# Nine row buffers instead of six and a later cut of the gather schedule in a hybrid decoder layer

## Chip, cores and metric

One Trainium2 chip, one core of it. The metric is the device time of one execution in microseconds; lower is better. Several executions are timed and their median is given; one more is profiled.

## The reference

One layer over 1024 tokens of width 1024, in float32: a token mixer (a short convolution group and a chunked gated DeltaNet group), cross-attention into 256 memory tokens, and a PEER channel mixer. The last one matters here. For each token it picks 8 x 16 = 128 of 16384 single-neuron experts and computes

```
u = expert_u[it]; v = expert_v[it]        # it: 128 expert numbers of each token
act = gelu(einsum("td,ted->te", xt, u))
y   = einsum("te,ted->td", gt * act, v)   # gt: 128 gates of each token
```

A final RMSNorm of the sum with the residual closes the layer.

## The kernel before

**Blocks and chunks.** The 1024 tokens are 8 blocks of 128. The mixer, the attention and the choice of experts run by chunks: `ca` (blocks 0 and 1), `cb` (2 to 5) and `cc` (6 and 7). The PEER mixer has two ways. Blocks 2 to 5 go the *dense* way (`densify`, lines 1025 to 1066, and `dense`, lines 1068 to 1143): a table of gates over all 16384 experts is made for each block by one-hot products on DVE and PE (the "tables"), and then all of `u_t` and `expert_v` are streamed past the 512 tokens. Each streamed tile `wraw` is split by ACT (`whi`, line 242) and DVE (`wlo`, line 244) for three matmuls (lines 248 to 250). Blocks 0, 1, 6 and 7 go by *gathers*: one indirect DMA of POOL's (line 918, or 964) fetches one expert row for each of 128 tokens, 128 x 4 KB, into one buffer `g`. The pool `gp` holds `NG` = 6 of these buffers, for U rows and V rows alike, and for the three tiles that `finish` (lines 992 to 1005) uses.

**What is done with a gathered row.** U rows are multiplied with the token and summed on DVE (line 935). V rows of blocks 1, 6 and 7 are weighted and added up on DVE (line 1020, the first on ACT, line 1018). V rows of block 0 go through PE (`gather_p`, line 971, into a PSUM bank `acc` that is copied to an SBUF slot `t_s` at line 983 and then to DRAM). `finish` loads the residual and the final gain, adds (999), squares on ACT (1001), takes an inverse root (lines 229 to 235, 12 small DVE instructions) and scales (1004).

```
915:  for k in range(NSLOT):
916:      ...
917:      g = gp.tile([P, D], F32, name="g")
918:      nc.gpsimd.indirect_dma_start(out=g, ...)
1016: for k, g in gathered("expert_v", r.ii, LV):
1020:     stt(y, g, a[:, k:k + 1], y, op0=OP.mult, op1=OP.add)
```

**What sets the order.** The parts are generators that yield after each step, and `merge` interleaves several of them in proportion to given weights. `gathers(0)` yields 3 steps for closing block 0's routing, 131 for block 0's U sums merged with block 1's closing, 256 for block 1's U sums merged with block 0's V rows (the close of block 0 is traced at the end of these), and 128 for block 1's V sums. The numbers `G1` to `G5` say how many of these steps are traced beside each part of the other work; what is left is merged with the dense stage, together with the 518 steps of blocks 6 and 7, against `PACE` = 517 dense steps:

```
1209: run(merge((steps(ga, G4), G4), (qb, 32), (steps(rest, C4), C4)))
1210: run(merge((steps(ga, G5), G5), (tables2, T5), (rest, 195 - C4)))
1213: run(merge((chain(ga, at('PG3', gathers(6))), 1036 - G1 - G2 - G3 - G4 - G5), (at("PD", dense(2 * P)), PACE)))
```

`tables2` closes the routing of blocks 2 to 5 (`route_close`) and makes their tables; `rest` is the mixer, the attention and `queries` of chunk `cc`, in that order. The order of tracing is a priority: a scheduler then sets the order of each engine's instructions, and pulls traced-later work forward where its operands and its buffer slots are there. Slots of a pool are given out in the order of tracing. The slots `t_s` (`NSLIP` = 4) are used by `best_keys` in `queries`, by `route_close` and by the copy at line 983. From the queries of `cb` on, `psum()` gives out the four `ps` banks only.

Of the kernel before, what the change touches and what calls it, by code (L numbers as in the profile page):

```python
# [39 lines left out]
CSTART = [sum(CAND[:r]) for r in range(16)]  # L40
NCAND = sum(CAND)
NSLIP, CLOSE, PACE = 4, 3, 517
G1, G2, G3, G4, G5 = 98, 90, 107, 17, 60
A5 = -1
C4, T5 = 61, 92
NSHORT, NRAW, NHI, NLO, NG, LU, LV, VD = 6, 3, 2, 2, 6, 1, 1, 194
PG1, PG2, PG3, PT, PR, PD = 100, -25, 0, 0, 0, 0


# [1205 lines left out]

# [10 lines left out]
```

## Time and profile before

| | us |
|---|---|
| median of 3 runs | 3342.78 (3332.52 to 3343.3) |
| profiled execution | 3335.89 |
| its span, first to last instruction | 3334.1 |
| PE busy in the span | 2784.7 (84%) |
| DVE busy | 2693.7 (81%) |
| ACT busy | 1339.8 (40%) |
| POOL busy | 1324.6 (40%) |

The share of 16 DMA engines' time that packets took is 44.3% for POOL's queue (the gathers) and 30.0% for SP's queue. A share over the whole span mixes stages with different limits, so the stages have to be read one by one. "Idle time, and what ended it" says for an engine which instruction of another engine or which DMA released the next instruction.

### The profile page before, as it was taken

To read this page: it belongs to the slowest core of one execution; us is meant where nothing else is said; L and a number is where in the kernel's file an instruction comes from. 1 tells how busy PE (TensorE), PEld (TensorE's weight loads), DVE (VectorE), ACT (ScalarE), POOL (GpSimd) and SP (SyncE) were. 2 spreads that over 40 slices of the span, in tenths; PEclk is the share of its full clock that TensorE was granted. 3 is DMA by queue.
4 is the path that set the end of the run, shared out by engine and by line. 5 is a ranking of instruction groups with operands and counts; after the bars stand their busy time and mean duration, and the time that the engine had idled before them with its cause. 6 is when DMAs were issued, how large, how long until landed. Compare 5 with 4: busy or idle time off the path is not lost.

```text
span 3334.1 us, 42650 instructions
## 1 busy us (share of the span) xinstructions
PE 2784.7 (84%) x14826; PEld 2307.0 (69%) x14826; DVE 2693.7 (81%) x5527; ACT 1339.8 (40%) x2367; POOL 1324.6 (40%) x1028
## 2 busy tenths in 40 slices
PE   7898588877888877466777999999999999999950
PEld 7887466666555656465656888888888888888840
DVE  6654899978655788997668999888888888887888
ACT  5444333322232323334443554444444444444430
POOL 0000046746545441000000456556655555665665
PEclk9999788989998888788788999999999999999975
DMA  4344368959988884113455889999999999999998
GB/s 166 113 147 140 120 233 302 354 184 324 328 309 306 308 291 155 64 77 143 154 190 188 297 307 363 347 344 346 345 336 342 348 348 349 343 339 339 348 329 315
DMA packets 325495, 890.34 MB, mean 267 GB/s; under 512 B 27424, under 2 KB 96672, under 8 KB 321184
## 3 DMA queue, kind: packets, MB, share of 16 engines
q0 software_dynamic: 147456, 536.94, 44.3%
q1 hardware_dynamic: 177824, 350.69, 30.0%
q8 instruction: 116, 1.90, 0.2%
q14 instruction: 99, 0.81, 0.1%
HBM read 838.77 MB, written 48.76 MB: 266 GB/s over the span
## 4 chain that ended last, share of the span: by engine, by line
PE 43%; DVE 3%; issue 2%; DMA 1%; ACT 1%; POOL 1%; SPq 0%; POOLq 0%; DVEq 0%; ACTq 0%
PE ps L248 7%; PE ps L249 7%; PE ps L250 7%; PE po L248 7%; PE po L250 7%; PE po L249 7%; DMA g<-expert_v,g_ii 1%; POOL g L918 1%; DVE unit L1053 0%; DMA d_s<-kmd 0%; PE ps L1059 0%; DVE g_y L1020 0%; DVE wlo L244 0%; ACT whi L242 0%; DVE unit L1050 0%
## 5 line engine op out<-in xcount | busy, mean ns | idle before, releaser
L918 POOL DMA_INDIRECT g<-expert_u,g_ii x512 | 666.4, 1302 | 898.9 <-DVE t_s L820 434.4
L918 POOL DMA_INDIRECT g<-expert_v,g_ii x384 | 518.5, 1350 | 930.8 <-ACT g L1001 536.0
L242 ACT ACTIVATE whi<-wraw 128x1024 fp32r<-128x1024 f32 x452 | 479.9, 1062 | 836.0 <-PE ps L249 413.5
L244 DVE TENSOR_TENSOR wlo<-wraw,whi 128x1024 fp32r<-128x1024 f32 x452 | 552.4, 1222 | 321.7 <-ACT whi L242 319.4
L935 DVE SCALAR_TENSOR_TENSOR g<-g,xn 128x1024 f32<-128x1024 f32 x512 | 617.4, 1219 | 121.0 <-DMA g<-expert_u,g_ii 111.7
L250 PE MATMUL ps<-unit,wlo 128*128 128x512 f32 (+1 forms) x1784 | 653.3, 367 | 39.4 <-DVE wlo L244 39.3
L248 PE MATMUL ps<-unit,whi 128*128 128x512 f32 (+1 forms) x1784 | 659.1, 370 | 13.7 <-ACT whi L242 5.5
L249 PE MATMUL ps<-unit,whi 128*128 128x512 f32 (+1 forms) x1784 | 651.6, 365 | 0.0
L1020 DVE SCALAR_TENSOR_TENSOR g_y<-g,g_a,g_y 128x1024 f32<-128x1024 f32 x381 | 488.1, 1281 | 20.1 <-DMA g<-expert_v,g_ii 12.7
L249 PE MATMUL po<-wlo,unit 128*128 128x512 f32 x1136 | 444.0, 391 | 0.0
L250 PE MATMUL po<-whi,unit 128*128 128x512 f32 x1136 | 443.9, 391 | 0.0
L250 PEld LDWEIGHTS ps<-unit,wlo 128*128 128x128 f32 x1784 | 350.3, 197 | 98.6 <-DVE wlo L244 45.0
L248 PEld LDWEIGHTS ps<-unit,whi 128*128 128x128 f32 x1784 | 351.6, 197 | 76.7 <-ACT whi L242 11.0
L249 PEld LDWEIGHTS ps<-unit,whi 128*128 128x128 f32 x1784 | 351.5, 197 | 50.0 <-issue 0.8
L248 PE MATMUL po<-whi,unit 128*128 128x512 f32 x1136 | 383.1, 391 | 0.0
L249 PEld LDWEIGHTS po<-wlo,unit 128*128 128x128 f32 x1136 | 214.1, 188 | 48.3 <-issue 2.7
L250 PEld LDWEIGHTS po<-whi,unit 128*128 128x128 f32 x1136 | 214.0, 188 | 46.8 <-issue 2.5
L248 PEld LDWEIGHTS po<-whi,unit 128*128 128x128 f32 x1136 | 214.0, 188 | 45.8 <-issue 1.1
L1113 ACT ACTIVATE unit<-po 128x512 f32<-128x512 f32 x256 | 152.6, 597 | 150.1 <-PE po L250 144.8
L964 POOL DMA_INDIRECT g<-expert_v,g_y x128 | 139.4, 1089 | 161.3 <-DVE g L935 57.5
L1100 ACT ACTIVATE po<-unit 128x512 f32<-128x512 f32 x248 | 144.5, 605 | 0.0
L1059 PE MATMUL ps<-unit 128*128 128x128 f16 x1024 | 86.8, 239 | 52.3 <-DVE unit L1053 38.7
(391 smaller groups left out, 4053.1 us busy)
## 6 DMA issues: line engine op xcount, KB each, us to landing
wraw<-u_t SPq DMA_DIRECT2D x128, 512.0 KB, 7.1
wraw<-expert_v SPq DMA_DIRECT2D x128, 512.0 KB, 7.0
wraw<-w_in SPq DMA_DIRECT2D x84, 512.0 KB, 4.6
gd<-unit SPq DMA_DIRECT2D x32, 1024.0 KB, 5.9
unit<-gd SPq DMA_DIRECT2D x32, 1024.0 KB, 15.1
wraw<-w_out SPq DMA_DIRECT2D x24, 512.0 KB, 4.2
wraw<-w_xq SPq DMA_DIRECT2D x24, 512.0 KB, 4.4
wraw<-w_xo SPq DMA_DIRECT2D x24, 512.0 KB, 4.9
```

What stands on the lines that cost most here:

```text
L242: act(hi, raw, AF.Copy)
L244: tt(lo, raw, hi.bitcast(F32), op=OP.subtract)
L248: nc.tensor.matmul(ps, lh, rh, start=first, stop=False, skip_group_check=open_)
L249: nc.tensor.matmul(ps, lh, rl, start=False, stop=False, skip_group_check=open_)
L250: nc.tensor.matmul(ps, ll, rh, start=False, stop=last, skip_group_check=open_)
L918: nc.gpsimd.indirect_dma_start(out=g, out_offset=None, in_=I[table], in_offset=bass.IndirectOffsetOnAxis(ap=ii[:, k:k + 1], axis=0))
L935: stt(g, g, 1.0, xn, op0=OP.mult, op1=OP.mult, accum_out=r.a[:, k:k + 1])
L964: nc.gpsimd.indirect_dma_start(out=g, out_offset=None, in_=I["expert_v"], in_offset=bass.IndirectOffsetOnAxis(ap=iT[:, t:t + 1], axis=0))
L1020: stt(y, g, a[:, k:k + 1], y, op0=OP.mult, op1=OP.add)
L1059: nc.tensor.matmul(ps[:, u * P:(u + 1) * P], part[i][:, g, :, t], oj[:, g, :, t], start=i == 0, stop=i == 1)
L1100: act(pss[b], y[b][:, half * 512:(half + 1) * 512], AF.Copy)
L1113: act(y[b][:, half * 512:(half + 1) * 512], pss[b], AF.Copy)
```

## The change

`NG` goes from 6 to 9: nine buffers `g` of 4 KB in each partition. The scratch that holds the descriptors of dynamic transfers is given as 4096 bytes of each partition. `G5` goes from 60 to 130: 70 more steps of `gathers(0)` are traced beside the tables and the rest of chunk `cc`, and 70 fewer beside the dense stage (the weight 664 in line 1213 becomes 594). Nothing that is computed changes.

```
-G1, G2, G3, G4, G5 = 98, 90, 107, 17, 60
+G1, G2, G3, G4, G5 = 98, 90, 107, 17, 130
...
-NSHORT, NRAW, NHI, NLO, NG, LU, LV, VD = 6, 3, 2, 2, 6, 1, 1, 194
+NSHORT, NRAW, NHI, NLO, NG, LU, LV, VD = 6, 3, 2, 2, 9, 1, 1, 194
...
-    nc = bacc.Bacc("TRN2", target_bir_lowering=False, num_devices=1)
+    nc = bacc.Bacc("TRN2", target_bir_lowering=False, num_devices=1, dynamic_dma_scratch_size=4096)
```

## Rows read from the trace of the kernel before

**Rows 1.** Stages: start:end, us, busy us (instructions) by engine, clock, DMA share, GB/s

```profile
434.00:667.00 233.00, 189.78 (x821) 150.95 (x821) 230.61 (x449) 79.02 (x124) 153.26 (x114) 0.91 0.89 318
667.00:1290.00 623.00, 505.37 (x2867) 375.19 (x2868) 449.49 (x1208) 176.20 (x363) 303.87 (x274) 0.88 0.80 288
1290.00:1500.00 210.00, 128.57 (x1007) 118.89 (x1005) 196.96 (x690) 76.87 (x176) 0.00 (x0) 0.79 0.20 77
1500.00:1800.00 300.00, 209.17 (x1570) 175.06 (x1570) 218.86 (x524) 131.06 (x341) 0.00 (x0) 0.84 0.46 168
...
1826.00:3210.00 1384.00, 1382.66 (x6099) 1144.22 (x6098) 1174.47 (x1459) 673.72 (x970) 787.47 (x570) 1.00 0.95 340
3210.00:3334.00 124.00, 0.66 (x3) 0.19 (x2) 106.96 (x145) 6.83 (x12) 77.88 (x66) 0.51 0.87 314
```

The engines stand in the order PE, PEld, DVE, ACT, POOL.

**Rows 2.** DVE's largest group from 3210 on; the chain's last sum

```profile
L1020 DVE SCALAR_TENSOR_TENSOR g_y<-g,g_a,g_y 128x1024 f32<-128x1024 f32 x71 | 91.1, 1284 | 11.0 <-DMA g<-expert_v,g_ii 10.1
...
3322.59 1.30 DVE g_y L1020
```

**Rows 3.** Waits in 1826 to 3210: us in total, times, longest

```profile
DVE g_y L1020 <- DMA g<-expert_v,g_ii: 2.5, 3, 1.1
...
POOL g L918 <- DVE g_y L1020: 241.1, 164, 5.3
POOL g L918 <- DVE g L935: 201.0, 116, 5.4
```

**Rows 4.** POOL's timeline around 1286 to 1822: start, us, [idle before, releaser]

```profile
1286.20 0.94 POOL L918 DMA_INDIRECT g<-expert_v,g_ii  x1 [9.19 <-DVE p_top L820]
1822.15 0.94 POOL L918 DMA_INDIRECT g<-expert_v,g_ii  x1 [535.02 <-ACT g L1001]
```

**Rows 5.** Timelines of ACT and PE ahead of the dense stage

```profile
1807.47 0.60 ACT L983 ACTIVATE t_s<-ps 128x512 f32<-128x512 f32 x1 [10.06 <-DVE p_topi L821]
...
1808.12 3.90 PE L293 MATMUL ps<-call,unit 128*128 128x128 f32 x16 [11.34 <-ACT t_s L983]
```

**Rows 6.** Waits of PE, DVE and POOL in 667 to 1290

```profile
PE po L971 <- DMA g<-expert_v,g_y: 31.5, 13, 9.1
PE ps L971 <- DMA g<-expert_v,g_y: 25.2, 8, 6.3
...
DVE g L935 <- DMA g<-expert_u,g_ii: 109.9, 63, 9.7
...
POOL g L964 <- DVE g L935: 57.5, 27, 7.1
POOL g L918 <- PE ps L971: 53.9, 14, 8.6
```

**Rows 7.** DVE's groups of sums in 1826 to 3210: busy us, mean ns

```profile
L1020 DVE SCALAR_TENSOR_TENSOR g_y<-g,g_a,g_y 128x1024 f32<-128x1024 f32 x310 | 396.9, 1280 | 9.1 <-ACT g_y L1018 4.5 <-DMA g<-expert_v,g_ii 2.5
...
L935 DVE SCALAR_TENSOR_TENSOR g<-g,xn 128x1024 f32<-128x1024 f32 x256 | 307.9, 1219 | 0.0
```

**Rows 8.** DVE's timeline of a close, first and last large instruction and one small

```profile
3323.91 1.23 DVE L999 TENSOR_TENSOR g_y<-g_y,g 128x1024 f32<-128x1024 f32 x1
...
3326.58 0.15 DVE L230 TENSOR_SCALAR rs_y<-rs_x 128x1 int32<-128x1 int32 x1
...
3328.57 1.28 DVE L1004 SCALAR_TENSOR_TENSOR g_y<-g_y,f_r,g 128x1024 f32<-128x1024 f32 x1
```

**Rows 9.** DMA: POOL's queue (packets, MB, share); issues of U rows (median landing us)

```profile
q0 software_dynamic: 147456, 536.94, 44.3%
...
g<-expert_u,g_ii POOLq DMA_INDIRECT x512, 7.0
```

**Rows 10.** Two stretches of 200 us in the dense stage, columns as in rows 1

```profile
2000.00:2200.00 200.00, 200.00 (x884) 165.58 (x884) 173.69 (x183) 95.68 (x139) 112.98 (x86) 1.00 0.98 356
...
2800.00:3000.00 200.00, 200.00 (x884) 165.63 (x883) 166.23 (x192) 94.81 (x138) 117.91 (x85) 1.00 0.96 343
```

**Rows 11.** The chain in 1600 to 1826, one of its pieces: start, us, what

```profile
1732.04 3.61 DVE unit L1053 x6
```

## The prediction, made before the changed kernel was run

> **What bounds the kernel now.** I read the stage table first [rows 1]. It shows three kinds of time. From 1826 to 3210 us, while the dense stage runs, PE is busy 1382.66 of 1384 us at full clock: there PE is the bound, and whatever is taken off DVE or the DMA queues only shows at the end. After 3210 PE has nothing left, and 124 us go to block 7's expert sums and what closes the kernel. Before 1826 no engine is full throughout: DVE is in 434 to 667 and in 1290 to 1500; elsewhere PE and DVE wait for each other. In 1290 to 1800 (the "tables") POOL does nothing and the DMA engines are busy 20 to 46%, so gathers could run there; DVE has 300 - 218.9 = 81 us of idle time in 1500 to 1800 and only 13 before that.
>
> Next the end, in the groups of DVE and the chain [rows 2]: 71 sums of line 1020 start after 3210, 1.284 us each, with 10.1 us of waiting for gathers, so (91.1 + 10.1) / 71 = 1.43 us a sum. The last starts at 3322.59, and 11.5 us of block 7's close follow. This is a backlog: PE finished while 71 sums had not been done.
>
> Then, who waits for whom in the dense stretch [rows 3]: POOL waits 241.1 + 201.0 us for DVE to free a row buffer, while DVE waits only 2.5 us for a gather. The gathers are held back by buffers and by the place of the sums in DVE's order, not by late data.
>
> POOL's timeline says why the tables have no gathers [rows 4]: the first of block 1's V rows are fetched by 1286, and the next one's issue waits 535.02 us for line 1001, the close of block 0. That close comes late for a small reason [rows 5]: the copy at line 983 needs a `t_s` slot, traced behind all of `queries(cc)`, and waits for its top-16 work (line 821). The copy is also what PE's transposes for the dense stage wait for, 11.34 us, because the sum of block 0 holds one of the four `ps` banks until then.
>
> Last, the stretch with block 0's V rows on PE, 667 to 1290 [rows 6]: PE waits 31.5 + 25.2 = 56.7 us for gathers and DVE 109.9 us, while POOL waits 57.5 us for line 935 and 53.9 us for line 971 to free a buffer. Here six buffers are too few for the landing time.
>
> **The change, part by part.**
>
> *130 steps instead of 60 beside the tables.* The steps before this merge are 98 + 90 + 107 + 17 = 312. Steps 1 to 390 are block 0 and block 1's U sums with block 0's V rows (3 + 131 + 256); POOL has issued all of those gathers by 1286 already, as block 1's V rows are under way by then [rows 4]. So of the 70 added steps 18 change nothing, and 442 - 390 = 52 of block 1's V sums really move, with block 0's close before them. The close is now traced at step 78 of 130, in `cross(cc)` and ahead of `queries(cc)`, so its `t_s` slot should come free once the four `route_close` of the tables are through.
>
> What it adds in the tables: 52 sums of 1.28 us on DVE [rows 7] = 66.6 us, and the close, 1.23 + 1.28 us and 12 small ones of 0.15 [rows 8] = 4.3 us: 71 us. Its gathers cost POOL and DMA time that lies idle there [rows 1]; ACT gets three instructions more, with over half its time idle; the stores of line 987, the close's three loads and its store pass through SP, ahead of weight loads: a load that waits there for a free `g` would hold these up, which nine buffers make unlikely. DVE takes its queue in order, so each sum stands ahead of whatever `cross`, `queries` or `densify` has ready. Bounds: 0, if all 71 us fall into the 81 us of idle time; 71, if none does. A sum put into a gap delays the next instruction by half its length on average, 52 x 0.64 = 33 us; the `ps` bank that is returned early takes a little off. I take +30.
>
> What it removes: 52 sums from the backlog, 52 x 1.43 = 74 us, leaving 71 - 52 = 19 sums and a tail of 124 - 74 = 50 us. This holds if the dense stretch goes on doing 310 + 256 = 566 sums [rows 7]. Should block 1's other 76 sums also be pulled forward, tables and tail trade nearly one for one. Bounds 0 (nothing moves) and 74 + 27 = 101 (the 19 go too).
>
> The early copy of line 983 removes PE's wait ahead of the dense stage [rows 5]: -11; bounds -11 and 0, since DVE's top-16 work is also in the way there.
>
> *Nine buffers.* In 667 to 1290 a gather can be issued three buffers earlier. POOL runs 274 instructions in those 623 us, nearly all of them gathers, one per 2.3 us [rows 1]; three of them are 6.8 us, about what one takes to land (7.0 us [rows 9]), and the longest waits are 9.1 and 9.7 us. I let two thirds of PE's wait go: 56.7 x 0.67 = -38. DVE's 110 us I don't add, as PE is the busier there (505 against 449 us of 623). Bounds: 0, if the sums are merely moved forward to meet the rows as late as before, and -57. In 434 to 667 DVE is full (230.6 of 233), so buffers give nothing.
>
> In the dense stretch nine buffers could raise the pace. The DMA engines move 340 GB/s on average there [rows 1], 356 from 2000 to 2200 and 343 from 2800 to 3000 [rows 10]. To take in the remaining 19 sums, of 128 rows x 4 KB = 0.524 MB each, they would need 340 + 19 x 0.524 MB / 1384 us = 347. The later stretch is the usual one, so I leave the 19 in the tail. The Trainium skill (DMA: Bandwidth & Descriptors, "Where 436 GB/s comes from") puts the HBM side of one core at about 358 GB/s. By that rule 347 is within reach, the 19 sums go, and the sum below is 27 us lower; by the rows it stands.
>
> *A scratch of 4 KB.* It frees 12 KB of each partition, the three added buffers of 4 KB. Nothing in the trace shows the scratch as such. In the trace, six transfers in flight run freely with the present size; bounds for the smaller one are 0 and a limit below six, priced as a rival. I take 0, as no gather there waits for anything but a buffer or POOL's own issue [rows 3].
>
> **The sum.** 3334.1 - 38 (early buffers) + 30 (tables) - 11 (dense start) - 74 (tail) = 3241 us span, and 1.8 us outside it as in the profiled execution (3335.89): **3243 us**. That execution was 6.9 us under the median of the three runs (3342.78); a median like theirs would be 3250, inside every range here.
>
> **Rivals.**
>
> *Better: all of it.* The 19 sums also fit into the dense stretch (-27) and PE loses all 57 us of waiting (-19 more): 3243 - 46 = 3197. For it: POOL's 442 us of buffer waits in the dense stretch. Against: the rate of the DMA engines. Chance 0.10.
>
> *The tables pay in full.* The chain in the tables has stretches of DVE alone, such as six table products in a row [rows 11]; if it is DVE's throughout, all 71 us show, and the buffers give nothing early. 3334 - 74 - 11 + 71 + 2 = 3322, faster by 0.4%, at the edge. Chance 0.13.
>
> *The change does not do what it says.* The close of block 0 still gets its slot only behind `queries(cc)`, and block 1's sums stay after 1807. Only the early buffers act: 3336 - 38 = 3298. Against: its place in the trace order is now ahead of `queries`. Chance 0.07.
>
> *Slower: the sums run ahead of the DMA engines in the dense stage.* With nine buffers the sums are put into DVE's order as closely as DVE allows. It has 1384 - 1174 = 210 us free [rows 1], room for 168 sums, so 734 in 1384 us, one per 1.89 us: 278 GB/s of gathers. The stage's own loads are 340 - 566 x 0.524 / 1.384 = 126 GB/s; 404 together against 356 at best [rows 10]. DVE then waits for rows with `wlo` behind it, and PE starves. The 585 gathers (307 MB) get 278 / 404 of 356, 245 GB/s: 1252 us, in which PE does 1252 x 356 / 404 = 1103 us of its work; 281 more follow. The stage takes 1533 instead of 1384 us, the backlog is gone: 3243 + 149 - 27 = 3365. It decides once PE's idle time in the stage passes about 95 us. For it: the 442 us. Against: DVE waits 2.5 us for gathers now, and the merge spreads 594 steps evenly over the dense stage. Chance 0.09.
>
> *Slower: the scratch holds too few transfers.* If fewer than six fit, gathers in the dense stage slow from one per 2.45 us: with two in flight at 7.0 us, one per 3.5, and 585 of them take 2050 us behind a start at 1826: over 3870 us in all. The queue's row gives 147456 packets for 1024 gathers, 144 each, 9 on each of 16 engines [rows 9]. The Trainium skill (the same page, "The descriptor swizzle" and "Terms") also has 9 descriptors per engine and 16 bytes for one; a ring of 4096 bytes on each engine would then hold an estimated 28 transfers, so this page speaks against the rival, and no run here shows it yet. Chance 0.03.
>
> **How the numbers follow.** The forecast has the rest, 0.58, with 3205 to 3290 by its bounds. A run tells a difference of about 0.3% (10 us) here. Faster: 0.58 + 0.10 + 0.07 + 0.08 of the full-price case = 0.83; same: its other 0.05; slower: 0.09 + 0.03 = 0.12. The range, 3180 to 3325, holds the forecast, most of the better case, the full price and the case that nothing moves; it leaves out both slower ones.
>
> **What would show it.** Right: block 0's close (line 999) and sums of line 1020 well before 1800; about 52 fewer sums of line 1020 after the last matmul, and a tail of 30 to 55 us; PE's waits for gathers at line 971 under 25 us; no 11 us wait at line 293. Wrong: a stretch from 1290 to the dense start longer by over 70 us; a wait of DVE for gathers in the dense stage well over 2.5 us with PE under 1.00 busy; POOL's first gather after 1290 still behind line 1001 near 1820; gathers landing later than now with POOL held at its issue.

## The result, and the profile after

The changed kernel is slower: 3413.43 us (3407.48 to 3422.61, four runs) against 3343.04 for the kernel before beside it, a ratio of 1.0225 with an interval of 1.0205 to 1.0244. The forecast was 3243 us, with a range of 3180 to 3325, so it missed in sign and the time lies outside the range. In the profiled executions the spans are 3408.8 and 3334.1 us: 74.7 us to explain.

Two marks cut this difference into three pieces: ACT's first instruction of the dense stage and PE's last matmul. First the timelines (start, length, engine, line) of the kernel before:

```profile
1825.85 1.28 ACT L1088 ACT_TABLE_LOAD   x1
...
3210.27 0.39 PE L250 MATMUL po<-whi,unit 128*128 128x512 f32 x1
```

The same of the kernel after:

```profile
1881.64 1.28 ACT L1088 ACT_TABLE_LOAD   x1
...
3384.75 0.39 PE L250 MATMUL po<-whi,unit 128*128 128x512 f32 x1
```

The dense stage starts 1881.64 - 1825.85 = 55.8 us later. It takes 1503.1 us for 1384.4, 118.7 more. What follows PE's last matmul is 24.1 us for 123.8, 99.8 less. The sum is 55.8 + 118.7 - 99.8 = 74.7. So the tail went, as forecast and more, and was paid for twice.

The stage table of the kernel after (columns as in [rows 1]) answers to that group:

```profile
434.00:667.00 233.00, 177.49 (x682) 139.38 (x681) 231.23 (x414) 65.49 (x90) 170.34 (x128) 0.84 0.94 345
667.00:1290.00 623.00, 546.97 (x3150) 404.84 (x3149) 464.31 (x1264) 200.98 (x412) 294.80 (x260) 0.92 0.77 286
1290.00:1500.00 210.00, 112.64 (x895) 103.23 (x894) 199.81 (x673) 71.89 (x177) 0.00 (x0) 0.75 0.18 67
1500.00:1800.00 300.00, 168.68 (x1218) 139.67 (x1218) 289.37 (x428) 108.39 (x295) 159.34 (x107) 0.75 0.88 324
...
1882.00:3385.00 1503.00, 1431.69 (x6098) 1157.83 (x6096) 1117.98 (x1428) 672.95 (x971) 717.33 (x512) 0.98 0.81 293
3385.00:3409.00 24.00, 0.14 (x1) 0.00 (x0) 17.88 (x72) 6.17 (x12) 0.00 (x0) 0.56 0.27 110
```

From 1500 to 1800 DVE is busy 289.4 of 300 us (before 218.9), and PE does 1218 matmuls for 1570. DVE's groups of sums say how much came in there: first 1290 to 1882, then 1882 to 3385.

```profile
L1020 DVE SCALAR_TENSOR_TENSOR g_y<-g,g_a,g_y 128x1024 f32<-128x1024 f32 x124 | 158.5, 1278 | 1.4 <-DMA g<-expert_v,g_ii 0.5
...
L1020 DVE SCALAR_TENSOR_TENSOR g_y<-g,g_a,g_y 128x1024 f32<-128x1024 f32 x257 | 329.9, 1284 | 3.3 <-DMA g<-expert_v,g_ii 1.2
```

Before 1882 there are 124 of block 1's 127 sums, not 52. The timelines of ACT, DVE and POOL show what released them (in brackets the idle time before and its end):

```profile
1491.72 0.58 ACT L983 ACTIVATE t_s<-ps 128x512 f32<-128x512 f32 x1
...
1500.61 1.22 DVE L999 TENSOR_TENSOR g<-g 128x1024 f32<-128x1024 f32 x1 [2.30 <-DMA g<-hd]
...
1503.28 0.94 POOL L918 DMA_INDIRECT g<-expert_v,g_ii  x1 [272.60 <-ACT g L1001]
```

The close of block 0 moved from about 1820 to 1500, as the prediction read from the order of tracing, and POOL's wait for it fell from 535.02 us [rows 4] to 272.60. From then on nothing held block 1's sums but DVE.

Next, the dense stage. A stretch of 800 us well inside it compares best; before:

```profile
2000.00:2800.00 800.00, 800.00 (x3531) 662.43 (x3531) 665.59 (x812) 383.67 (x557) 466.05 (x340) 1.00 0.97 347
```

After:

```profile
2000.00:2800.00 800.00, 749.07 (x3155) 601.85 (x3154) 698.07 (x872) 342.98 (x498) 545.97 (x388) 0.97 0.99 364
```

388 gathers for 340, and 3155 matmuls for 3531: 10.6%, or 85 of 800 us, are lost. 51 us of them are idle time of PE; the other 34 are PE's busy time per matmul, which grew. The granted clock, 0.97 on average for 1.00, makes some 22 us of these (0.03 x 749); the other 12 the profile does not explain. The DMA engines are busy 0.99 of the time at 364 GB/s. The waits of 1882 to 3385 (in total, times, longest) name what PE stands at:

```profile
ACT ps L1088 <- PE ps L250: 242.7, 73, 5.0
...
POOL g L918 <- DVE g_y L1020: 130.1, 109, 7.6
...
POOL g L918 <- DVE g L935: 66.2, 54, 3.9
...
PE po L248 <- ACT whi L242: 40.3, 17, 5.3
...
ACT whi L242 <- DMA wraw<-expert_v: 26.1, 13, 5.4
...
PE ps L250 <- DVE wlo L244: 17.8, 24, 3.2
...
DVE g L935 <- DMA g<-expert_u,g_ii: 3.5, 2, 2.5
```

POOL's 442 us of waiting for buffers [rows 3] are down to 196. PE waits for the two halves of the weight tiles. ACT, which makes the first half, waits for the tiles themselves too, but for 26.1 us where it was 18.7 before, so this wait alone does not explain the loss. DVE still hardly waits for a gather. The chain from 2100 to 2900 has five weight loads among its pieces, 92 us in all (before, it has PE's matmuls alone), for instance:

```profile
2204.57 19.40 DMA wraw<-expert_v
...
2405.16 18.36 DMA wraw<-expert_v
...
2647.78 20.57 DMA wraw<-expert_v
```

From 2000 to 2900 the median tile of `expert_v` lands in 7.9 us (before 7.0); these are the late ones.

Late tiles are the smaller part of it, though. The timelines of ACT and PE show wait by wait what a late `whi` stood behind. Of PE's 51 us of idle time from 2000 to 2800, 13 follow a tile that had only just landed:

```profile
2668.43 1.06 ACT L242 ACTIVATE whi<-wraw 128x1024 fp32r<-128x1024 f32 x1 [3.56 <-DMA wraw<-expert_v]
...
2669.54 2.07 PE L248 MATMUL po<-whi,unit 128*128 128x512 f32 x4 [5.29 <-ACT whi L242]
```

Some 36 follow a `whi` that had to wait its turn on ACT. Its tile had landed (in PE's waits for `whi`, 1.8 to 11 us before, once 0.1), but in ACT's queue it stands behind the gelu of line 1088, or the copy of line 1113, of the tile that PE is still working on. ACT waits for PE to end that tile, and PE then waits for ACT:

```profile
2077.57 0.58 ACT L1088 ACTIVATE ps<-ps 128x512 f32<-128x512 f32 x1 [4.86 <-PE ps L250]
2078.06 1.05 ACT L242 ACTIVATE whi<-wraw 128x1024 fp32r<-128x1024 f32 x1
...
2079.16 1.19 PE L248 MATMUL po<-whi,unit 128*128 128x512 f32 x4 [1.63 <-ACT whi L242]
```

Before, from 2000 to 2800, the next tile's `whi` always stands ahead of these:

```profile
2323.47 1.06 ACT L242 ACTIVATE whi<-wraw 128x1024 fp32r<-128x1024 f32 x1 [2.01 <-PE ps L249]
2324.44 0.58 ACT L1088 ACTIVATE ps<-ps 128x512 f32<-128x512 f32 x1
```

In the same 800 us the changed kernel's queue has 24 places where it stands behind. So nine buffers changed the written order of ACT's queue as well as that of DVE's. Why the scheduler wrote it so, no run shows.

Behind 3000 all gathers are done, the stage runs at 874 matmuls per 200 us with the DMA engines at 119 GB/s to the end: the gathers were hurried through a stage that would have had room for them.

### The profile page after: what moved, and what is told of

Its sections match the earlier page's. It is cut to its first block, busy times and chain, and to the rows that moved or that the text cites. A ratio compares the mean times of both kernels' runs of the same rounds, so it can differ in the third digit from the quotient of the medians.

```text
span 3408.8 us, 42651 instructions
## 1 busy us (share of the span) xinstructions
PE 2843.5 (83%) x14826; PEld 2321.7 (68%) x14826; DVE 2695.9 (79%) x5527; ACT 1338.6 (39%) x2367; POOL 1362.1 (40%) x1028
## 4 chain that ended last, share of the span: by engine, by line
PE 34%; DVE 8%; DMA 5%; issue 3%; ACT 2%; POOL 0%; DVEq 0%; ACTq 0%; POOLq 0%
PE ps L250 6%; PE ps L248 6%; PE ps L249 6%; PE po L249 5%; PE po L250 5%; PE po L248 5%; DMA wraw<-expert_v 3%; DVE g_y L1020 2%; DVE wlo L244 2%; ACT whi L242 1%; DVE g L935 1%; DMA g<-expert_v,g_ii 1%; DVE unit L1053 0%; DMA d_s<-kmd 0%; DMA wraw<-w_pq 0%
## 5 line engine op out<-in xcount | busy, mean ns | idle before, releaser
L918 POOL DMA_INDIRECT g<-expert_u,g_ii x512 | 692.7, 1353 | 815.1 <-DVE t_s L820 520.2
L249 PE MATMUL po<-wlo,unit 128*128 128x512 f32 x1136 | 455.3, 401 | 3.2 <-DVE wlo L244 2.5
L250 PE MATMUL po<-whi,unit 128*128 128x512 f32 x1136 | 452.2, 398 | 0.0
L248 PE MATMUL po<-whi,unit 128*128 128x512 f32 x1136 | 390.2, 398 | 40.3 <-ACT whi L242 40.3
L250 PEld LDWEIGHTS po<-whi,unit 128*128 128x128 f32 x1136 | 218.9, 193 | 48.9 <-issue 3.4
L964 POOL DMA_INDIRECT g<-expert_v,g_y x128 | 147.9, 1156 | 172.8 <-DVE g_y L949 75.0
L1088 ACT ACTIVATE ps<-ps 128x512 f32<-128x512 f32 x128 | 74.3, 580 | 242.7 <-PE ps L250 242.7
L250 PE MATMUL po<-unit,wlo 128*128 128x256 f32 (+1 forms) x360 | 127.3, 353 | 39.7 <-DVE wlo L244 39.7
```

The lines of the kernel that those rows point to most:

```text
L248: nc.tensor.matmul(ps, lh, rh, start=first, stop=False, skip_group_check=open_)
L249: nc.tensor.matmul(ps, lh, rl, start=False, stop=False, skip_group_check=open_)
L250: nc.tensor.matmul(ps, ll, rh, start=False, stop=last, skip_group_check=open_)
L918: nc.gpsimd.indirect_dma_start(out=g, out_offset=None, in_=I[table], in_offset=bass.IndirectOffsetOnAxis(ap=ii[:, k:k + 1], axis=0))
L964: nc.gpsimd.indirect_dma_start(out=g, out_offset=None, in_=I["expert_v"], in_offset=bass.IndirectOffsetOnAxis(ap=iT[:, t:t + 1], axis=0))
L1088: act(ps, ps, AF.Gelu)
```

## The experiments

All are edits of the kernel before; NG is the number of row buffers, G5 the cut, "scratch" the 4096 bytes of the changed kernel. In the first four expectations theory A means the buffers (they set the pace of the gathers); later it means the bytes on the DMA engines, as each says.

**Parts of the change alone.** Nine buffers without the cut:

```
-... NSHORT, NRAW, NHI, NLO, NG = 6, 3, 2, 2, 6
+... NSHORT, NRAW, NHI, NLO, NG = 6, 3, 2, 2, 9    (and the scratch)
```

> The changed kernel's buffers and scratch with the old cut of 60. Theory A (the buffers set the pace): in the dense stage the gathers run at about 50 per 100 us instead of 42.5, the DMA engines carry 365 to 375 GB/s, weight loads land late now and then, and PE does 8 to 11% less while that lasts; 638 gathers take about 1280 us, so the dense stage is some 120 us longer and the backlog of 71 sums is gone: about 3340 to 3370 us, ratio 1.00 to 1.01. Theory B (the emptier DVE after the cut sets the pace): the pace stays at 42 to 43 and PE at 1.00 busy, the backlog stays near 70 sums, and only the 15 us before the tables are gained: about 3320, ratio 0.995.

Measured: 3368.75 us, ratio 1.0094 (1.0065 to 1.0123). The dense stage starts 11 us earlier than before (1814.80), and the 800 us inside it look like those of the changed kernel:

```profile
2000.00:2800.00 800.00, 744.69 (x3138) 597.33 (x3138) 696.66 (x863) 341.06 (x497) 552.13 (x390) 0.97 0.99 366
```

So the buffers alone make the dense stage slow: it takes 1524.8 us, 140.4 more than before, and leaves no sum behind it. Between this kernel and the changed one lies the cut, by which the dense stage starts 66.8 us later (1881.64 - 1814.80) and is 21.7 us shorter.

The cut alone (G5 = 130, six buffers, the old scratch):

> Only the cut: 130 steps, six buffers, the scratch as before. Theory A: block 1's sums go into the tables as in the changed kernel (about 127 of them before the dense stage, which starts 50 to 75 us later than before), but the dense stage keeps its pace of 42.5 gathers per 100 us and PE at 1.00 busy for 1384 us; 512 gathers take 1205 us, so no backlog is left and the end comes about 30 us after PE's last matmul: 3300 to 3320 us, ratio 0.985 to 0.995. Theory B: the pace rises to 50 without the buffers, PE loses 100 us and more: 3390 to 3420, ratio 1.015 to 1.025.

Measured: 3327.18 us, ratio 0.9965 (0.9950 to 0.9979). From 1500 to 1800:

```profile
1500.00:1800.00 300.00, 164.94 (x1238) 139.79 (x1238) 279.65 (x424) 110.34 (x297) 150.77 (x92) 0.77 0.79 289
```

113 sums of line 1020 run ahead of the dense stage, which starts at 1898.97, 73.1 us late; from 2200 on PE is full again (884 matmuls per 200 us at 348 GB/s), and no sum is left behind its last matmul. Tables and tail trade against each other, and the cut is worth 0.35%.

The scratch alone (six buffers, G5 = 60):

> Only the scratch of 4096 bytes; six buffers, 60 steps. Both theories: the same order of instructions, and the time of before within 0.3% (3333 to 3353). Rival (the small scratch holds transfers back): gathers land later than 7 us or POOL takes longer for one than the 1.30 to 1.36 us of before, and the time is longer by 1% or more.

Measured: 3332.96 us, ratio 0.9986 (0.9973 to 0.9999). It costs nothing, which removes the rival of a scratch too small. The Trainium skill's page (DMA: Bandwidth & Descriptors, "The descriptor swizzle" and "Terms"), from which the prediction had estimated 28 transfers of room, agrees. The run shows that six transfers fit, not how many would.

Intermediate cuts with six buffers, G5 = 80 and G5 = 100:

> Six buffers, 80 steps: block 0's close is traced beside the tables, and only 2 of block 1's sums are. If the close's slot is what held block 1's sums back, all of them run in the tables here too, and the time is that of the cut at 130 within 0.5%. If the place in the order of tracing decides, only a few sums move: dense start 5 to 15 us earlier than before, backlog near 70, about 3325 us.

> Six buffers, the scratch of before, the cut at 100: the close of block 0 is traced at step 78 of 100, two thirds of the way to the end of the merge and more. If the place of the close in the order of tracing decides, there are two outcomes: either it lies ahead of the queries and then, as with the cut at 130, block 1's sums are pulled forward as far as DVE lets them, 100 or more ahead of 1900, dense start 1885 to 1905, 3315 to 3335 us; or it still lies behind and nothing moves, 75 sums after the last matmul, 3333 to 3343 us. If the number of steps decides instead (the reading of the prediction), 22 sums move, dense start 1835 to 1850, some 50 sums left after the last matmul, 3315 to 3330 us.

Measured: 3335.46 us, ratio 0.9992 (0.9982 to 1.0003), with 4 sums ahead of the dense stage; and 3318.65 us, ratio 0.9953 (0.9935 to 0.9970), with 113 of them, the stage starting at 1903.64. Of the expectation for 80 neither branch came true as a whole: few sums moved, but the stage started at 1832.70, 7 us later than before and not 5 to 15 earlier. That for 100 held. How many steps are traced beside the tables does not decide. Where the close of block 0 stands among them does: behind the queries nothing moves, ahead of them nearly everything does. With 80 the close is step 78, at the end of the merge.

**How many buffers, and how many weight tiles.**

```
-... NRAW, NHI, NLO, NG = 3, 2, 2, 6
+... NRAW, NHI, NLO, NG = 3, 2, 2, 8    (or 7; or NRAW 4 and NG 8; and the scratch)
```

> Eight row buffers, scratch 4096, cut at 60 as before, three weight buffers. Both theories take it as the point between six buffers (ratio 1.000) and nine (1.009 with the cut at 60). Theory A (each buffer beyond six raises the pace of the gathers in the dense stage, and the DMA engines, full by then, bring the weight tiles late): more than 93 gathers per 200 us between 2000 and 2800, PE 183 to 195 of 200 us there, 3350 to 3365 us. Rival (the harm comes with the ninth buffer alone, for instance by an order that the scheduler happens to find): PE 198 or more of 200, 85 to 90 gathers per 200 us, 3300 to 3343 us.

> Seven row buffers, scratch 4096, three weight buffers, the cut at 60. In the program as it is written, DVE's queue has 2.45 sums per weight tile in most of the dense stage (before 2.31, eight buffers 2.66, nine 3.03), and 41 sums behind the last tile (before 74, eight and nine none). Theory A (each tile needs 1 + n loads of 0.524 MB in the 5.4 us that PE takes for it, and about 20 GB/s of other loads; PE is slowed only where that passes the 366 to 375 GB/s that the DMA engines reached): 2.45 sums need 355 GB/s, so PE stays at 198 or more of 200 us from 2000 to 3000, the dense stage ends near 3200, 41 sums x 1.4 us and the close follow, 3265 to 3285 us. Theory B (any order with more sums between the tiles than before delays wlo and costs PE): PE at 192 to 197 of 200, 3290 to 3320 us.

> As the kernel with eight row buffers and the cut at 60, and one weight buffer wraw more (four for three). Theory A1 (DMA engines can carry both streams on average; PE starves since single weight loads land 16 to 20 us after their issue and only three are in flight): with four in flight PE comes back to at least 196 of 200 us between 2000 and 2800 at a pace of 90 or more gathers per 200 us, DMA 365 GB/s or more, waits of PE for whi and wlo fall from some 50 us to under 20, and the time is 3260 to 3320 us. Theory A2 (the engines are simply full, or DVE's order delays wlo): PE stays at 183 to 195 of 200, the time within 15 us of the kernel with eight buffers and three weight buffers.

Measured: eight buffers 3296.69 us, ratio 0.9891 (0.9862 to 0.9920); seven 3304.38, ratio 0.9890 (0.9864 to 0.9917); eight with four weight tiles 3306.39, ratio 0.9910 (0.9884 to 0.9936). The same 800 us, eight buffers:

```profile
2000.00:2800.00 800.00, 766.19 (x3301) 618.34 (x3300) 683.54 (x845) 355.83 (x518) 517.01 (x370) 0.99 0.98 358
```

Seven:

```profile
2000.00:2800.00 800.00, 785.44 (x3426) 643.13 (x3426) 674.85 (x829) 370.61 (x540) 491.44 (x354) 1.00 0.97 352
```

Eight with four weight tiles:

```profile
2000.00:2800.00 800.00, 800.00 (x3532) 662.40 (x3530) 669.23 (x822) 382.80 (x553) 459.93 (x341) 1.00 0.97 347
```

With 6, 7, 8 and 9 buffers there are 340, 354, 370 and 390 gathers in these 800 us and 3531, 3426, 3301 and 3138 matmuls. Eight buffers did better in total than expected (3350 to 3365): PE loses 79 us in the stage, and the backlog is gone. Seven did worse than expected (3265 to 3285), with PE at 785 where 792 was forecast, and 36 sums behind the last matmul. The fourth weight tile brought PE back, but not as its theory had it: the scheduler then writes DVE's queue with the old ratio of sums to tiles, and ACT's with no `whi` behind a gelu, the pace of the gathers falls back to 341, and 68 sums are left.

That ratio goes with the pace in all four. Sums (lines 935 and 1020) per weight tile (line 244), counted in DVE's groups of these 800 us, are (199 + 139) / 147 = 2.30 before, 2.49 with seven, 2.69 with eight, (230 + 157) / 132 = 2.93 after. It is set when the program is built: the written queues, as the expectations count them, have 2.31, 2.45, 2.66 and 3.03 for six to nine buffers, and the trace has about the same. More buffers let the scheduler place a sum earlier, ahead of the next weight tile.

**What a higher ratio costs: bytes or DVE.** Two kernels halve the bytes of the gathers of blocks 6 and 7; they leave out half of each row.

```
-indirect_dma_start(out=g, in_=I[table], ...)
+indirect_dma_start(out=g[:, :512], in_=I[table] as half rows, ...)
-stt(y, g, a[:, k:k + 1], y, ...)
+stt(half of y, g[:, :512], ...) twice;   or once, reading g[:, :512] two times
```

> Nine buffers, scratch 4096, cut at 60. Leaves out: for blocks 6 and 7 each gather fetches half of a row (2 KB for each of 128 tokens), and DVE works on that half twice, so DVE's work stays about the same while these gathers move half the bytes; what is summed is other data. Until about 2150 us block 1's full rows still run. Theory A (DMA engines are what PE starves on): from 2300 on PE is busy 197 or more of 200 us at a pace of at least 90 sums per 200 us, with DMA below 300 GB/s; no gathers are left over and the time is 3230 to 3300 us. Theory B (DVE's sums stand ahead of wlo in its queue, DMA is incidental): PE stays at 180 to 192 of 200 and the time at 3340 to 3390 us, with PE's waits naming wlo.

> Nine buffers, scratch 4096, cut at 60. Leaves out: for blocks 6 and 7 each gather fetches half of a row, and DVE reads that half twice in one instruction of the same 1024 columns (the product of U rows is written as bfloat16 beside it), so a sum costs DVE what it cost, and its gather half the bytes. The written order has 3.00 sums per weight tile from tile 96 to tile 160 (some 2370 to 2750 us), as nine full rows have (3.03), 4.5 per tile in the 32 tiles before those, and 2.5 and fewer after them. Theory A (bytes): with 3.00 half rows a tile needs about 265 GB/s, so PE is at 196 or more of 200 us between 2450 and 2700 where the kernel with nine full rows has 183 to 184, and 3260 to 3300 us in all. Theory B (the order of DVE's queue alone): PE stays at 180 to 190 of 200 in that stretch, 3310 to 3360 us. In the 32 tiles with 4.5 sums DVE is over its time in both theories.

Measured: 3302.38 us, ratio 0.9916 (0.9890 to 0.9941), and 3444.19 us, ratio 1.0318 (1.0282 to 1.0354). In the first, PE did no better in these 800 us than with nine full rows (3167 matmuls for 3138), with the DMA engines busy 0.79 of the time and DVE fuller than with full rows (736 us for 697):

```profile
2000.00:2800.00 800.00, 747.28 (x3167) 594.82 (x3166) 735.77 (x1462) 343.56 (x500) 474.62 (x399) 0.99 0.79 261
```

The second is slower than nine full rows, with its DMA engines busy only 0.75 of the time:

```profile
2000.00:2800.00 800.00, 672.01 (x2693) 529.21 (x2692) 668.33 (x838) 291.92 (x424) 543.51 (x394) 0.93 0.75 245
```

Its largest DVE group shows why (last column: idle time and its end):

```profile
L939 DVE SCALAR_TENSOR_TENSOR g<-g,xn 128x1024 bf16<-128x1024 f32 x231 | 278.0, 1222 | 115.0 <-DMA g<-expert_u,g_ii 113.7 <-DMA xn<-xnd 0.6 <-issue 0.2
```

The scheduler wrote 394 sums to 112 tiles, 3.5 per tile, and DVE stood 115 us in front of rows that had not landed, with `wlo` behind them. So PE can also starve with DMA time to spare, by DVE's order. This is no undoing of bytes at a fixed order, and the pair settled nothing about nine full rows.

The next five leave the gathers alone and load one resource each: six buffers, G5 = 60, the scratch. Loads of one tile's size are put behind weight tiles, or a subtraction on DVE:

```
         tt(lo, raw, hi.bitcast(F32), op=OP.subtract)
+        if dense stage and tile number % 4:
+            nc.sync.dma_start(junk, 128 rows of expert_v)      (three junk tiles)
+            tt(junk[:, :1], junk[:, :1], lo[:, :1], ...)       (the "tied" kernels only)
+        or:  tt(junk, raw, hi.bitcast(F32), op=OP.subtract)    (the DVE kernel)
```

> The kernel before (six buffers, cut 60, scratch 4096) and, behind three of every four weight tiles of the dense stage, one more load of 0.524 MB on SP's queue into a tile that nobody reads. DVE's written order stays that of before (2.31 sums per tile), and a tile then costs the DMA engines 1 + 2.31 + 0.75 = 4.06 loads, nearly what it costs with nine buffers (1 + 3.03 = 4.03). Theory A (bytes): the stage asks for 345 + 0.75 x 0.524 / 5.4 us = 418 GB/s; at the 366 to 375 reached before PE falls to 0.88 to 0.91, that is 770 to 805 matmuls per 200 us for 884, and the time rises by 120 to 190 us, 3460 to 3530 us. Theory B (DVE's order alone): PE stays at 198 or more of 200, 3330 to 3365 us.

> As the kernel with loads behind three of four tiles, but behind one of three: 1 + 2.31 + 0.33 = 3.64 loads per tile, as with eight buffers (1 + 2.66). Theory A: 345 + 32 = 377 GB/s asked for, PE at 190 to 199 of 200, the time 10 to 60 us above before, 3350 to 3400 us. Theory B: PE at 198 or more, 3330 to 3350 us.

Measured: ratios 1.0093 (1.0066 to 1.0121) and 0.9992 (0.9980 to 1.0004). They told nothing of the stage (the first one's loss lies ahead of it, as it starts 39 us later): nothing held the added loads back, all 187 of the first kernel were issued between 9.9 and 438.7 us, and from 2000 to 2800 its DMA engines stayed at 344 GB/s.

> The kernel before (six buffers, cut 60, scratch 4096) and, behind three of every four weight tiles of the dense stage, one more subtraction of 128x1024 on DVE into a tile that nobody reads: DVE's time per tile becomes 1.73 + 2.25 x 1.165 + 0.75 x 1.14 = 5.2 us of PE's 5.4, as with nine buffers (1.73 + 3.03 x 1.165 = 5.26), at no byte more for the DMA engines. In the written order 98 sums stand behind the last tile (before 74). Theory A (bytes): PE stays at 198 or more of 200 at 340 GB/s, the dense stage ends near 3210 and 98 sums x 1.4 us follow: 3360 to 3390 us. Theory B (DVE is too full for an engine that works in order): PE at 175 to 192 of 200 and 3440 to 3540 us.

> The earlier kernels with added loads sent them off ahead of the stage, so they told nothing. Here each added load (0.524 MB, SP's queue, three tiles of their own, six row buffers, scratch 4096, cut 60, behind three of four weight tiles) is read by a DVE instruction of one column that also reads wlo of its tile, so the next loads can't start before the stage has come there. The written order falls to 2.0 sums per weight tile and 143 sums behind the last: DVE needs 1.73 + 2.0 x 1.165 + 0.75 x 0.1 = 4.1 us of PE's 5.4, less than before (4.4). Bytes: 1 + 2.0 + 0.75 loads per tile, 3.75 x 0.524 / 5.4 + 20 = 384 GB/s asked for. Theory A (bytes): at the 366 to 375 GB/s reached before PE falls to 0.95 to 0.98, 840 to 866 matmuls per 200 us, DMA at 360 GB/s or more, dense stage 1410 to 1455 us. Theory B (DVE alone): PE 884 matmuls per 200 us, DMA at 380 or more, dense stage 1384 us. About 143 x 1.43 us of sums and the close follow in both.

> As the kernel with tied loads behind three of four tiles, but behind every tile: 1.96 sums per tile in the written order, DVE 4.1 of 5.4 us, and 1 + 1.96 + 1 = 3.96 loads per tile, 404 GB/s asked for, nearly what nine buffers ask for (4.03 loads). Theory A: PE at 0.90 to 0.93, 800 to 822 matmuls per 200 us at 360 to 375 GB/s, dense stage 1490 to 1540 us, with PE's waits naming whi and ACT's naming the loads of wraw. Theory B: PE 884 matmuls per 200 us, DMA above 390 GB/s, dense stage 1384 us.

Measured, the added subtractions: 3414.07 us, ratio 1.0217 (1.0192 to 1.0242), between the two expectations in the stage:

```profile
2000.00:2800.00 800.00, 782.05 (x3399) 637.68 (x3398) 755.68 (x882) 368.57 (x536) 505.36 (x324) 1.00 0.94 330
```

DVE at 755.7 of 800 us, at 330 GB/s, costs PE 3.7% of its matmuls. Of its 84 us over before, 50 lie in the stage (1828.45 to 3262.61) and 32 behind it, with 94 sums left. So a full DVE costs PE too, but a third as much as what nine buffers do. ACT's wait for weight tiles is no sign that tells causes apart: over these 800 us it is 78.3 us here, 20.7 after and 13.3 before. Measured, the tied loads: 3545.57 us, ratio 1.0618 (1.0597 to 1.0638), behind three of four tiles, and 3640.28 us, ratio 1.0912 (1.0884 to 1.0939), behind all. Three of four:

```profile
2000.00:2800.00 800.00, 767.27 (x3306) 622.52 (x3304) 583.52 (x798) 358.55 (x519) 359.99 (x273) 0.99 0.99 364
```

All:

```profile
2000.00:2800.00 800.00, 738.55 (x3085) 583.67 (x3084) 550.18 (x779) 331.67 (x485) 345.81 (x254) 0.98 0.98 359
```

And what the latter's PE waits for:

```profile
PE po L256 <- ACT whi L244: 26.3, 15, 3.4
...
PE ps L256 <- ACT whi L244: 20.4, 22, 2.8
...
PE ps L258 <- DVE wlo L246: 12.8, 25, 0.5
```

As a count, demand and supply look like this. At full speed PE takes 147 tiles in 800 us, so one load of 0.524 MB per tile is 96.3 GB/s; before, 3.30 loads a tile are 318, and 347 - 318 = 29 GB/s are other transfers. The kernel after wants 3.93 loads a tile, 407 GB/s; it gets 364, and 132 of 147 tiles. Tied loads behind every tile want 1 + 1.95 + 1 = 3.95 loads, 409 GB/s; they get 359, and 130 tiles, with DVE busy 69% of the time instead of 87%. At three of four, 3.72 loads want 387 GB/s and get 364: 0.94, and the matmuls are 0.936. That these shares agree proves nothing by itself: with the loads per tile fixed by the written order, bytes and tiles fall together whatever holds PE.

So a loss as large comes with DVE less busy than before the change, and a full DVE is not needed for it. But that bytes alone make it is not shown. The tied loads changed ACT's written order too:

```profile
2416.45 0.58 ACT L1097 ACTIVATE ps<-ps 128x512 f32<-128x512 f32 x1 [4.86 <-PE ps L258]
2416.95 1.05 ACT L244 ACTIVATE whi<-wraw 128x1024 fp32r<-128x1024 f32 x1
...
2418.05 0.50 PE L256 MATMUL po<-whi,unit 128*128 128x512 f32 x1 [1.63 <-ACT whi L244]
```

With loads behind every tile, 60 of PE's 61 us of idle time lead back to such an instruction of ACT's that waits for PE, and ACT waited 0.2 us for a weight tile; with three of four it is 25 of 32, and 7 for late tiles. The expectation that ACT's waits would name the loads of `wraw` failed. Counted from 2000 to 2800, the places where `whi` stands behind, and the matmuls lost:

| kernel | places | matmuls lost |
|---|---|---|
| before | 0 | 0 |
| seven buffers | 9 | 3.0% |
| eight buffers | 16 | 6.5% |
| nine buffers, cut 60 | 21 | 11.1% |
| after | 24 | 10.6% |
| eight buffers, four weight tiles | 0 | 0 |
| tied loads, three of four | 19 | 6.4% |
| tied loads, all | 40 | 12.6% |
| added subtractions | 0 | 3.7% |

Places and GB/s asked for broadly rise together in all of these but the last, so no run separates the order from the bytes. One would have to keep ACT's order of before at nine buffers' pace of gathers. The added loads also go through SP's queue, like the weight tiles, and the gathers through POOL's, so even the late tiles of the two need not be late for one reason. PE lost more than expected with the tied loads, with 826 and 771 matmuls per 200 us for 840 to 866 and 800 to 822.

**The cut, once the buffers cost little.** Seven buffers with G5 = 90 and 92, eight with 90:

> As the kernel with seven buffers and the cut at 60, with the cut at 90: in the written order 11 more sums stand ahead of the dense stage (268 for 257) and 34 for 41 behind the last tile. If sums pulled into the tables cost what they save (after: 127 moved for +71 us net of the early gain, 0.56 us each; six buffers and the cut at 130: +73 us), the time is within 8 us of the kernel with the cut at 60; if only the first ones are cheap since DVE has idle time there, 8 to 15 us better; if worse than 8 us, the close of block 0 itself is what costs in the tables.

> Seven buffers, scratch 4096, the cut at 92 for 90. In the written order 378 sums stand ahead of the dense stage (268 with the cut at 90 or 91) and none behind its last tile: two steps decide over 110 sums, since the close of block 0 then gets its slot ahead of the queries. If each sum ahead of the stage costs some 0.57 us there (six buffers: 73 us for 127), the stage starts some 60 us later than with the cut at 90 (first gelu of the stage near 1885), PE's loss in the stage is gone or small, 34 sums x 1.4 us are gone from the end: 3290 to 3320 us. If sums ahead of the stage are cheap, 3240 to 3280 us.

> Eight buffers, scratch 4096, cut at 90: in the written order 11 more sums stand ahead of the dense stage than with the cut at 60, 2.7 per tile in it, none behind it. Theory A (bytes): 2.7 x 0.524 / 5.4 + 0.524 / 5.4 + 20 = 379 GB/s asked for, PE at 188 to 195 of 200, and the time within 10 us of the kernel with eight buffers and the cut at 60 (ratio 0.989). If the 11 sums are as cheap as with seven buffers (0.989 to 0.986), ratio 0.985 to 0.988.

Measured: 3297.51 us, ratio 0.9859 (0.9823 to 0.9895); 3328.15 us, ratio 0.9963 (0.9950 to 0.9976); 3309.86 us, ratio 0.9921 (0.9897 to 0.9945). With 90, 12 sums run ahead of a dense stage that starts at 1826.30, and 29 are left behind PE's last matmul. Two steps more, and 121 run ahead of a stage that starts at 1885.44: 59.1 us for 109 sums, 0.54 us each, and no tail of 29 sums makes up for it. The third lies at the edge of the 10 us from the kernel with eight buffers and G5 = 60 that theory A gave it (10 by the ratios, 13 by the medians); the 12 sums ahead of the stage were not cheap there, as it starts 15.8 us later. Seven or eight buffers without the long cut beat both kernels, that of before by 0.8 to 1.4%; which of them is best, the intervals don't tell.

## Why the prediction was wrong

**The dense stage at 0: the step that failed.** The prediction kept the pace of 566 sums in 1384 us, since the DMA engines' later stretch [rows 10] left no room, and let 19 sums stay in the tail; it gave the nine buffers no cost there. The chip did not refuse the extra sums: they were written into DVE's queue ahead of the weight tiles, the gathers went ahead of them, and the halves of the weight tiles came late to PE. The term is +118.7 us, and the nine-buffer kernel without the cut shows that the buffers make it. How they do is shown in part: by the trace, 36 of 51 us of PE's idle time come of ACT's written order and 13 of tiles that landed late. Whether the bytes would cost as much without that order stays open.

**The rival with 0.09** had the extra demand and nearly the size: 404 GB/s asked for (407), 356 served (364), a stage of 1533 us (1503). Its argument against, that the merge spreads 594 steps evenly, took the order of tracing for the order of the queues. Its path is not the one that the trace shows: it let DVE wait for rows with `wlo` behind it, and DVE waited 4.7 us for them in all; PE waited for `whi`, mostly behind ACT's own order. It also put 585 sums into the stage, where 513 were done, so that its nearness is in part luck. Its 3365 us lay 48 under the measured time, mostly since the stage started 75 us later than it had assumed, against 30 us by which its stage was too long.

**The tables, +30.** The price per sum was right, the count wrong. 30 us for 52 sums is 0.58 us each; measured are 66.8 / 124 = 0.54 (after against nine buffers) and 73.1 / 113 = 0.65 (six buffers). But with the close of block 0 done by 1500 the scheduler pulled up 124 sums. The prediction named this case in a sentence and did not price it. The stage starts 56 us later, where 30 - 38 - 11 = -19 had been forecast. Of these 75 us, 37 lie here (66.8 for 30), 27 in the early buffers and 11 in the dense start.

**The early buffers, -38.** PE's waits for gathers at line 971 fell as forecast, from 56.7 us [rows 6] to the 19.5 of these waits of the kernel after:

```profile
PE po L971 <- DMA g<-expert_v,g_y: 11.8, 5, 4.3
...
PE ps L971 <- DMA g<-expert_v,g_y: 7.7, 2, 5.4
```

But the gain did not reach the dense stage. From 667 to 1290 PE did 3150 matmuls for 2867, and half of these 283 only made up for 434 to 667, where PE did 682 for 821. There DVE is full, and with nine buffers it spent more on U sums (149 us for 133), so the buffers cost something where the prediction had "nothing". The rest was gone by 1500, behind the stretch in which DVE is full again (199.8 of 210 us from 1290): with nine buffers and the cut at 60, the trace has 7097 matmuls of PE up to then, for 7096 before. With the cut at 60 the dense stage starts 11 us earlier with nine buffers, 16 with seven and 21 with eight, not 38.

**The dense start, -11.** Line 983's copy now comes at 1491.72, and PE's wait for it is gone. The gain did not show: the copy moves together with the sums, and the net of the two is +66.8 us.

**The tail, -74.** It fell by 99.8 us, the upper bound of 101 in all but a microsecond, since no sum was left.

**The scratch, 0.** Right: 0.9986 alone.

**The 27 us more by the page.** The prediction gave a rule of the Trainium skill (DMA: Bandwidth & Descriptors, "Where 436 GB/s comes from"), about 358 GB/s for the HBM side of one core, by which 347 would be within reach. The averages of 800 us that full DMA engines gave here, 359 to 366, lie 0.3 to 2.2% above it. The rate of 347 was in reach, and 364 was reached, but not at PE's full pace.

## What to carry to other kernels

Before giving a stream of prefetches more buffers, count what it will then ask of the shared engines per unit of the stage's bound work (here loads per weight tile), and compare the sum with the rate that the profile shows with those engines full. Near that rate single loads of the stage come late: seven buffers ask for 365 GB/s by this count, and PE already lost 3.0%. Then look at the order that the other engines' queues got: an instruction that makes the next tile ready must stand ahead of the one that waits for the present tile. A cut in an order of tracing is no count of steps that move: look for the slot or the result whose place releases everything behind it, and price the case that all of it moves. Work that ends early in a stage whose resource it shares has been bought from that stage, so aim for both to end together.

## What the runs showed that was not expected

More row buffers changed the order of an engine that hardly touches the rows: ACT's queue got 24 places in 800 us where the next tile's split stands behind work on the present one. With eight buffers it has 16, and a fourth weight tile took them all away. Full DMA engines gave 359 to 366 GB/s over 800 us in five kernels, above the 356 over 200 us that the prediction had called the best; a 200 us stretch after reached 372. In that state single weight loads stood 16 to 21 us in the chain while the median landing rose by less than one (7.9 for 7.0): the median says nothing of the loads that hold PE. When PE began to have gaps, its granted clock went from 1.00 to 0.97, worth some 22 of the 85 us lost. And giving a weight stream one more buffer slowed another stream, from 370 to 341 gathers in 800 us, through the written order alone.
